# A diffusion transformer block on one core: gate modulation by quarters in the up projection, a written order at the end, input weights loaded one ahead

## The chip, the cores and the metric

The kernel runs on one core of a Trainium2 chip. The core has the TensorE (PE) for matmuls, the VectorE (DVE) and ScalarE (ACT) for elementwise work, the GpSimd (POOL, here almost only an issuer of DMAs) and the SyncE (SP, here only an issuer of DMAs), all of which run their own instruction streams in order and wait for each other by semaphores. The metric is the device time of one execution in microseconds (us). A profiled execution gives, beside it, every instruction with its start and its duration.

## What is computed

One layer of a hybrid diffusion backbone, for 512 latent tokens and 256 context tokens of width 2048, all in float32. Cut to what matters here:

```python
mod_l = silu(c) @ w_ada + b_ada              # 6 x 2048: sh_a, sc_a, gt_a, sh_f, sc_f, gt_f
mod_c = silu(c_ctx) @ w_ada + b_ada          # only sh_a, sc_a are needed
h_l = rms_norm(x, g_mix_norm) * (1 + sc_a) + sh_a
p   = h_l @ w_in                             # 3904 columns: attention and short conv
x   = x + gt_a * (merge_heads(att, conv) @ w_out)
h_f = rms_norm(x, g_ffn_norm) * (1 + sc_f) + sh_f
u   = dwconv3(h_f @ w_up)                    # 2 x 5504 columns
x   = x + gt_f * ((a * silu(g)) @ w_down)    # a, g = halves of u
out = rms_norm(x, g_final)
```

The modulation is six vectors of 2048 numbers for the latent tokens. In the kernel they are 96 tiles t of 128 numbers: 0 to 15 are sh_a, 16 to 31 sc_a, 32 to 47 gt_a, 48 to 79 sh_f and sc_f, and 80 to 95 gt_f, the gate behind the down projection.

## The kernel before

Features lie on the 128 partitions, tokens on the free axis. A float32 value is split into a rounded high part (cast on ACT) and the rest (subtracted on DVE), and each product is three matmuls: high by high, high by low, low by high (`mm3`, L183 to L185). So every weight block that comes by DMA costs a cast on ACT (L166, L984) and a subtraction on DVE (L167, L985) before the PE can use it. Tile names end in h and l accordingly.

The modulation is no matmul. A tile of 128 x 2048 of w_ada is loaded and multiplied on DVE with `sv`, the silu of c on all partitions, and summed along the row (a "dot"; two instructions of 128 x 1024 a tile, L229, L251, or four of 128 x 512, L1234). There are three places: `ada` (L229) in the input projection for t < 32, `late_dot` (L251) during attention and the out projection for t = 32 to 87, and `gate_mods` (L1234) in the first part of the down projection for t = 88 to 95, by quarters of 512, with `sv` read back from a DRAM copy `sv_d`. The context's own dots (L510) use `svc`, the silu of c_ctx.

The stages in order of time, with their rough place in the span:

- **Start** (0 to 28 us). SP issues the loads of c, the 16 tiles of x (xr), c_ctx, small constants, then w_ada and the first weights. `silu_rows` spreads c and c_ctx over all partitions by matmuls with ones and applies Silu on ACT (L393, L394). Squares of x are summed on DVE (15 adds, L335), `rms` turns them into the row `rl`: matmuls with ones (L300), square root on ACT (L277, with a load of its function table), reciprocal on DVE (L279), a transpose on the PE that spreads it (L284), a copy (L307). `modulate(j)` multiplies xs[j] by rl (L415), applies scale and shift on ACT (L418) and splits the result into h{j}h and h{j}l.
- **Input projection** (28 to about 600 with attention). w_in is taken in row chunks of 2, 4 and 10 tiles (`KCH`). In each chunk the first six column blocks (`pf`, weights `rf`) run beside the preparation of h; then the other 25 (`pp`, weights `rw`) follow, and each result is added into `acc` (L519, L521). A weight tile is loaded by `load` just where it is used, into one of two buffers of 1 MB (three with a spare one). The calls are written in program order, and `todo` says which h is prepared behind which block.
- **Out projection** (to about 808). Residual and squares of the new x tile by tile (`residual`, L943); the norm of the second half of the tokens waits for the last tile.
- **Up projection** (813 to 1676). The first three pairs of column blocks are done whole (`uf`), then for f = 3 to 42 a scheme of seven products (`product`, names p1, p2, p6, q5, p7 and q4, q3 of the round before, in `finish`) over 1024-wide weights `u`. Two of its five weight blocks are sums that the DMA makes by accumulating into SBUF (L1107). `acts` is the convolution and the gating, `pair_sums` (L1028 to L1047) makes sums of pairs and writes them out to `t_d`. Such background work lies in the queue `bg`, and `pump` takes one step of it behind each product. The rounds have nine weight buffers (`raw4`) and three split buffers each.
- **Down projection** (1676 to 2141). First seven tiles plainly (`d`), then 48 steps of seven products (`seven`, names v{st}p1 and so on) over windows of six pairs. `into` adds each result to its output tile `c` (L1319), from step 8 on times the gate. The last two steps, v22 and v23, are written out by hand.
- **End** (to 2156). Squares of the outputs, the final norm (L300, L277, L279, L284), `scale_out` (ACT, L1393) and `final`: the product with the norm on DVE (L1386) and the writes of 256 KB, 8 for each half of the tokens, issued from SP and ACT.

Within this code the framework's scheduler orders each engine's stream by priority in program order and modelled times, except where `keep` or an `issue_after` fixes one instruction behind another.

## Time and profile before

| | us |
|---|---|
| median of 3 runs | 2158.14 (2150.28 to 2158.75) |
| the profiled execution | 2158.0 |
| its span (first to last instruction) | 2156.2 |
| PE busy | 2104.1 |
| DVE busy | 1770.6 |
| ACT busy | 1046.8 |
| mean granted clock of the PE | 0.992 |

The span is what the trace shows from the first to the last instruction; 1.8 us of the execution lie outside it. The PE's busy time nearly fills the span, so the idle pieces, and the stretches with a granted clock below 1, are what to look at. The rows that matter are quoted in the prediction.

### The profile page before, as it was taken

The numbers are of one execution on the slowest core, as the hardware profiler recorded it, in microseconds if no ns is written. First come the engines' busy times: TensorE is split into PE (matmuls) and PEld (weight loads), VectorE is DVE, ScalarE is ACT, GpSimd is POOL, SyncE is SP. The second block draws the span as 40 slices with busy tenths as digits, with TensorE's granted clock in tenths as the row PEclk, the third lists the DMA queues.
The fourth block names the chain that finished last, engine by engine and source line by source line (L and its number), as shares of the span: only waits on it lengthen the run. The fifth ranks groups of instructions, "written<-read, shape, count | busy, mean of one in ns | idle before, by whom it ended". The sixth has DMA issues, their size and how long they took to land.

```text
span 2156.2 us, 37750 instructions
## 1 busy us (share of the span) xinstructions
PE 2104.1 (98%) x14458; PEld 1946.8 (90%) x14458; DVE 1770.6 (82%) x2859; ACT 1046.8 (49%) x1709; POOL 188.1 (9%) x270
## 2 busy tenths in 40 slices
PE   7999999999999999999999999999999999999996
PEld 4788788888988888999999999999999889999996
DVE  7998987778886989788888888788888659888886
ACT  5533333555542237555555555555555333333445
POOL 0000000000000000111111111111111000000000
PEclk9999999999999999999999999999999999999998
DMA  9989885334559986677877877887877998877773
GB/s 338 348 274 334 268 284 177 130 125 157 181 198 345 357 272 187 160 216 201 242 230 215 239 225 223 239 235 214 238 229 219 345 331 289 260 217 235 210 234 110
DMA packets 162409, 513.89 MB, mean 238 GB/s; under 512 B 18994, under 2 KB 23346, under 8 KB 156594
## 3 DMA queue, kind: packets, MB, share of 16 engines
q1 hardware_dynamic: 132564, 417.10, 56.7%
q0 software_dynamic: 27488, 92.29, 18.2%
q8 instruction: 113, 1.85, 0.3%
q10 hardware_dynamic: 2176, 2.10, 0.3%
q14 instruction: 68, 0.56, 0.1%
HBM read 464.22 MB, written 46.14 MB: 237 GB/s over the span
## 4 chain that ended last, share of the span: by engine, by line
PE 90%; DVE 4%; DMA 3%; ACT 2%; issue 1%; SPq 0%; DVEq 0%; ACTq 0%
PE pp L183 4%; PE pp L185 4%; PE pp L184 4%; PE o L183 1%; PE o L184 1%; PE o L185 1%; PE d L183 1%; PE d L185 1%; PE d L184 1%; PE uf L183 1%; DMA ada<-in_w_ada 1%; PE uf L184 1%; PE uf L185 1%; PE of L183 1%; PE of L184 1%; PE of L185 1%
## 5 line engine op out<-in xcount | busy, mean ns | idle before, releaser
L1030 POOL DMA_DIRECT2D t_d<-tp x126 | 71.8, 573 | 469.1 <-DVE tp L1029 466.7
L251 DVE SCALAR_TENSOR_TENSOR ada<-ada,sv 128x1024 f32<-128x1024 f32 x68 | 82.1, 1220 | 13.5 <-DMA ada<-in_w_ada 13.5
L166 ACT CAST w_0h<-rw 128x512 fp32r<-128x512 f32 (+1 forms) x63 | 38.3, 618 | 106.2 <-PE pp L184 65.4
L1107 POOL DMA_DIRECT2D u_s<-in_w_up x80 | 70.2, 877 | 225.2 <-DMA u_s<-in_w_up 109.8
L229 DVE SCALAR_TENSOR_TENSOR ada<-ada,sv 128x1024 f32<-128x1024 f32 x64 | 77.6, 1219 | 3.8 <-DMA ada<-in_w_ada 3.6
L510 DVE SCALAR_TENSOR_TENSOR ada<-ada,svc 128x1024 f32<-128x1024 f32 x64 | 76.0, 1220 | 2.8 <-DMA ada<-in_w_ada 2.8
L1028 ACT CAST tp<-a 128x256 fp32r<-128x256 f32 x90 | 34.7, 404 | 63.2 <-DMA t_d<-tp 51.8
L773 POOL TENSOR_TENSOR gr<-gr,half 128x8 f32<-128x8 f32 x4 | 10.1, 2522 | 627.8 <-DVE gr L772 535.8
L167 DVE TENSOR_TENSOR w_0l<-rw,w_0h 128x512 fp32r<-128x512 f32 (+1 forms) x63 | 42.6, 682 | 21.7 <-ACT w_0h L166 21.7
L251 DVE SCALAR_TENSOR_TENSOR ra<-ra,sv 128x1024 f32<-128x1024 f32 x44 | 52.5, 1219 | 1.4 <-DMA ra<-in_w_ada 1.3
L1199 DVE TENSOR_TENSOR u<-u,u_s 128x1024 f32<-128x1024 f32 x40 | 48.8, 1220 | 1.1 <-DMA u_s<-in_w_up 1.0
L1200 DVE TENSOR_TENSOR u<-u,u 128x1024 f32<-128x1024 f32 x40 | 48.7, 1218 | 0.0
L1029 DVE TENSOR_TENSOR tp<-a,tp 128x256 fp32r<-128x256 f32 x90 | 36.2, 418 | 13.8 <-ACT tp L1028 13.7
L744 ACT CAST pth<-t 128x384 fp32r<-128x384 f32 x64 | 28.6, 485 | 26.5 <-PE t L741 26.5
L521 DVE TENSOR_TENSOR acc<-acc,pp 128x512 f32<-128x512 f32 x50 | 34.0, 681 | 2.1 <-PE pp L185 2.1
L745 DVE TENSOR_TENSOR ptl<-t,pth 128x384 fp32r<-128x384 f32 x64 | 33.3, 550 | 2.7 <-ACT pth L744 2.7
L1028 ACT CAST tp<-ts 128x256 fp32r<-128x256 f32 x36 | 14.6, 407 | 41.5 <-DMA t_d<-tp 39.6
L725 DVE TENSOR_REDUCE mn<-s 128x1 f32<-128x768 f32 x32 | 30.4, 953 | 4.7 <-PE s L714 4.6
L1029 DVE TENSOR_TENSOR tp<-ts,tp 128x256 fp32r<-128x256 f32 x36 | 15.2, 422 | 22.3 <-ACT tp L1028 22.3
L991 ACT ACTIVATE g<-cg,sm 128x512 f32<-128x512 f32 x40 | 32.5, 813 | 0.6 <-DVE cg L1168 0.6
L991 ACT ACTIVATE a<-ca,sm 128x512 f32<-128x512 f32 x40 | 32.1, 803 | 0.0
L999 ACT ACTIVATE g<-g 128x512 f32<-128x512 f32 x43 | 27.1, 631 | 6.4 <-DVE g L993 6.4
(15965 smaller groups left out, 9401.3 us busy)
## 6 DMA issues: line engine op xcount, KB each, us to landing
ada<-in_w_ada SPq DMA_DIRECT2D x196, 512.0 KB, 6.0
u<-in_w_up SPq DMA_DIRECT2D x120, 512.0 KB, 8.3
w<-t_d SPq DMA_DIRECT2D x161, 256.0 KB, 5.3
u_s<-in_w_up SPq DMA_DIRECT2D x80, 512.0 KB, 4.2
u_s<-in_w_up POOLq DMA_DIRECT2D x80, 512.0 KB, 9.1
t_d<-tp POOLq DMA_DIRECT2D x126, 256.0 KB, 4.9
v<-in_w_dnw SPq DMA_DIRECT2D x72, 384.0 KB, 5.4
ra<-in_w_ada SPq DMA_DIRECT2D x22, 1024.0 KB, 4.9
```

Source lines behind the costliest of these rows:

```text
L183: PE.matmul(ps, w[0], x[0], start=first, stop=False, skip_group_check=on_top)
L184: PE.matmul(ps, w[0], x[1], start=False, stop=False, skip_group_check=on_top)
L185: PE.matmul(ps, w[1], x[0], start=False, stop=last, skip_group_check=on_top)
L229: V.scalar_tensor_tensor(out=r, in0=r, scalar=1.0, in1=vec[:, i * 1024:(i + 1) * 1024], op0=ALU.mult, op1=ALU.mult, accum_out=col[:, i:i + 1])
L251: keep(V.scalar_tensor_tensor(out=r, in0=r, scalar=1.0, in1=svs[i], op0=ALU.mult, op1=ALU.mult, accum_out=lc[:, t % 4:t % 4 + 1] if i else ...
L510: keep(V.scalar_tensor_tensor(out=raw[q], in0=raw[q], scalar=1.0, in1=svc[:, q * 1024:(q + 1) * 1024], op0=ALU.mult, op1=ALU.mult, accum_o ...
L991: A.activation(u, src, AF.Identity, bias=s("fb", m), scale=s("fw", 86 + m))
L1028: A.copy(out=z[:, :256], in_=src)
L1029: V.tensor_tensor(out=z[:, 256:], in0=src, in1=z[:, :256].bitcast(F32), op=ALU.subtract)
L1030: G_.dma_start(t_d[p, OPS.index(n)], z.bitcast(F32))
L1107: G_.dma_start(r[-1], src[more], accum_op=ALU.add)
L1199: V.tensor_tensor(out=a11, in0=a11, in1=s1, op=ALU.add)
```

## The change

Three groups of edits.

**Modulation.** `late` ends at tile 80 instead of 88, so eight tiles (16 dots, 8 MB) leave the out projection. `gate_mods` now covers all 16 gate tiles and is stepped in the up projection: `product` calls `between`, which takes a step of `bg` or, where none waits, the next quarter. There are 64 loads of 256 KB and 64 dots of 128 x 512, through one buffer (tag "ts", shared with the temporary of `pair_sums`), and rl is reused for the quarter of sv. The down projection's 32 quarters and their four loads of sv are gone. sv_d is written in the out projection instead of right at the start.

**Input projection.** The silu of c_ctx leaves the start: c_ctx is loaded on all partitions and goes through one Silu of 128 x 2048 in the second chunk. The squares make two sums of eight tiles, with 14 adds. The first dots (tiles 16 and 0) and the first scaling are put in a written order around the reciprocal. Weights come from `weights()`, which issues the load after the one that it hands out, ahead of the `modulate` and `prep` calls that follow.

**End.** The a12 and s3 of the last step get buffers of their own, a square root of a constant is put on ACT behind the casts of q4, and outs, squares and statistics are fixed in one written order; the first half's writes are all issued from SP.

```diff
-    late = {"t": 32, "raw": None, "end": 88}
+    late = {"t": 32, "raw": None, "end": 80}
...
+        def prep_first():
+
+            a = first_dot(1, 0, recips[0].ins)
+            with tc.issue_after(a):
+                b = V.tensor_tensor(out=xs[0], in0=xs[0], in1=rl, op=ALU.mult).ins
+            first_dot(1, 1, b)
+            low_after[:] = [total(first["col"][1], 0, mod[:, 0:1]).ins]
...
-        silu_rows(c_ctx, svc, "cc")
         fetch_to(sm, small)
-        rms([ssq], D, T, rl)
+        first_scale()
+        ahead.append(first["last"])
+        rms(sqs, D, T, rl)
...
+        def weights(ahead=True):
+
+            raw = ready.popleft()
+            if ahead:
+                load_next()
+            return raw
...
-                    prep(q)
+                    prep(q) if q else prep_first()
+                    if q:
+                        load_next()
...
-                    raw = load(w_in[:, off:off + 2 * G * P], 2 * G * P, f"rf{ci}{q}")
+                    raw = weights(ci > 0)
...
+    def gate_mods():
+
+        for q in range(4):
+            SP.dma_start(rl, sv_d[:, q * T:(q + 1) * T])
+            for i in range(16):
+                r = cp.tile([P, T], F32, tag="ts", bufs=1, name=f"aq{i}{q}")
+                SP.dma_start(r, w_ada[80 + i][:, q * T:(q + 1) * T])
+                yield
+                V.scalar_tensor_tensor(out=r, in0=r, scalar=1.0, in1=rl, op0=ALU.mult, op1=ALU.mult, accum_out=parts[q // 2][:, i, q % 2:q % 2 + 1])
...
+    def between():
+
+        if bg:
+            pump(1)
+        else:
+            next(gm, None)
+
     def product(ps, a, n, nm, first):
...
-        pump(1)
+        between()
...
+        own = ("12", "s3") if st == STEPS - 1 else ()
...
+    with tc.issue_after(last_hi[0]):
+        A.activation(tiny(1, "root"), eps, AF.Sqrt)
+    pump(1)
+    d_q5(za, (3,))
     squares(za.m + 1, H1)
-    pump(2)
-    d_q5(zb)
+    d_q5(zb, (1,), lambda: [keep(next(outs)) for _ in range(2)])
+    keep(last_into[0])
     squares(zb.m + 1, H1)
-    pump(1)
     scaled = {j: scale_out(j, 1) for j in range(0, za.m, 2)}
-    for _ in range(3):
-        next(outs)
+    keep(next(outs))
     d_q3(za)
```

How the streams move, at three places. SP at the start, from the first weights on; before (rf and rw are weights of w_in, ada modulation loads, sv_d the copy of sv):

```order
L145 DMA rf_251<-in_w_in 128x1536
L972 DMA sv_d<-sv 128x2048
L145 DMA ada_283<-in_w_ada 128x1024
L145 DMA ada_285<-in_w_ada 128x1024
L145 DMA ada_291<-in_w_ada 128x1024
L145 DMA ada_293<-in_w_ada 128x1024
L145 DMA rw_13_337<-in_w_in 128x2048
L145 DMA ada_360<-in_w_ada 128x1024
L145 DMA ada_362<-in_w_ada 128x1024
```

Six further ada loads follow there, and then the second load rw. After (here all weights of w_in are named rw):

```order
L145 DMA rw_226<-in_w_in 128x1536
L145 DMA ada_274<-in_w_ada 128x1024
L145 DMA ada_276<-in_w_ada 128x1024
L145 DMA ada_282<-in_w_ada 128x1024
L145 DMA ada_284<-in_w_ada 128x1024
L145 DMA rw_298<-in_w_in 128x2048
L145 DMA rw_330<-in_w_in 128x2048
L145 DMA ada_353<-in_w_ada 128x1024
L145 DMA ada_355<-in_w_ada 128x1024
```

The second and the third rw now stand together behind the first four ada loads that follow the first weights, and the copy of sv is gone from this place.

DVE in the up projection, in the round f = 7 (g, a, ca, cg are convolution and sums, names in l the low parts); before:

```order
L318 TENSOR_TENSOR yh5l<-a_9248,yh5h 128x512
L1200 TENSOR_TENSOR u_12_9109<-u_12_9109,u_11_9107 128x1024
L985 TENSOR_TENSOR u6q4l<-u_22_8870,u6q4h 128x1024
L1210 SCALAR_TENSOR_TENSOR ca_9123<-u6c,u_9345 128x256
L985 TENSOR_TENSOR u6q3l<-u_12_8862,u6q3h 128x1024
L1198 TENSOR_TENSOR cg_9363<-u7b,u_9393 128x256
L985 TENSOR_TENSOR u7p6l<-u_11_9107,u7p6h 128x1024
L985 TENSOR_TENSOR u7q5l<-u_s_9111,u7q5h 128x1024
L1168 TENSOR_TENSOR cg_9122<-u6c,u_9286 128x256
L985 TENSOR_TENSOR u7p7l<-u_s_9114,u7p7h 128x1024
```

After, the same piece with the quarter dots aq:

```order
L1247 SCALAR_TENSOR_TENSOR aq_9754,modc<-aq_9754,rl 128x512
L338 TENSOR_TENSOR yh5l<-a_9213,yh5h 128x512
L1069 TENSOR_TENSOR u6q3l<-u_12_8812,u6q3h 128x1024
L1311 TENSOR_TENSOR cg_9328<-u7b,u_9361 128x256
L1069 TENSOR_TENSOR u7p6l<-u_11_9060,u7p6h 128x1024
L1247 SCALAR_TENSOR_TENSOR aq_9787,modc<-aq_9787,rl 128x512
L1069 TENSOR_TENSOR u7q5l<-u_s_9064,u7q5h 128x1024
L1281 TENSOR_TENSOR cg_9075<-u6c,u_9251 128x256
L1069 TENSOR_TENSOR u7p7l<-u_s_9067,u7p7h 128x1024
L1076 SCALAR_TENSOR_TENSOR g_9461<-cg_9075,sm,g_9461 128x511
L1076 SCALAR_TENSOR_TENSOR a_9466<-ca_9076,sm,a_9466 128x511
L1247 SCALAR_TENSOR_TENSOR aq_9818,modc<-aq_9818,rl 128x512
```

Three dots stand in this piece, each on the same buffer, so that the load for one is issued behind the dot before it; the splits keep their order among each other.

ACT in the last steps, around v23p6h, which the PE needs first of v23's later products (out are the scalings of finished output tiles); before:

```order
L1393 ACTIVATE out_23729<-c_18805,sm 128x256
L1393 ACTIVATE out_23729<-c_18807,sm 128x256
L1393 ACTIVATE out_23732<-c_18809,sm 128x256
L1393 ACTIVATE out_23732<-c_18811,sm 128x256
L1393 ACTIVATE out_23735<-c_18813,sm 128x256
L1393 ACTIVATE out_23735<-c_18815,sm 128x256
L1393 ACTIVATE out_23738<-c_19124,sm 128x256
L1393 ACTIVATE out_23738<-c_19126,sm 128x256
L1393 ACTIVATE out_23741<-c_19130,sm 128x256
L984 CAST v23p6h<-v_23326 128x768
L984 CAST v22p7h<-v22s_23132 128x768
L984 CAST v23p7h<-v23s_23329 128x768
```

After:

```order
L1490 ACTIVATE out_23766<-c_18893,sm 128x256
L1490 ACTIVATE out_23769<-c_18895,sm 128x256
L1490 ACTIVATE out_23769<-c_18897,sm 128x256
L1490 ACTIVATE out_23772<-c_18899,sm 128x256
L1490 ACTIVATE out_23772<-c_18901,sm 128x256
L1490 ACTIVATE out_23775<-c_18903,sm 128x256
L1068 CAST v23p6h<-v_23360 128x768
L1490 ACTIVATE out_23775<-c_18905,sm 128x256
L1490 ACTIVATE out_23778<-c_19172,sm 128x256
L1490 ACTIVATE out_23778<-c_19174,sm 128x256
L1068 CAST v22p7h<-v22s_23166 128x768
L1490 ACTIVATE out_23781<-c_19178,sm 128x256
```

Before, 15 scalings stand between v21q3h and v23p6h; after, 11 do, and the others follow it.

164 lines of the change are left out of this document (105 added, 59 removed).

## The prediction

> **What bounds the kernel now.** I read the page's first part, then the busy time in stretches, then the waits of the PE, and last the rows around the long waits.
>
> ```profile
> PE 2104.1 (98%) x14458; PEld 1946.8 (90%) x14458; DVE 1770.6 (82%) x2859; ACT 1046.8 (49%) x1709; POOL 188.1 (9%) x270
> ```
>
> The PE has work in all but 2156.2 - 2104.1 = 52.1 us of the span. No matmul of the model's layers is removed by the change, so all that it can win is a part of these 52 us, and time in which the PE runs at a lower clock. The stretches (PE, PEld, DVE, ACT, POOL busy, then granted clock, DMA share, GB/s) say where they lie:
>
> ```profile
> 0.00:20.00 20.00, 12.24 (x14) 4.34 (x15) 11.19 (x19) 14.81 (x25) 0.20 (x4) 1.00 0.91 329
> 20.00:40.00 20.00, 15.29 (x44) 9.71 (x44) 17.59 (x36) 9.09 (x15) 0.00 (x0) 1.00 0.93 367
> 40.00:60.00 20.00, 16.92 (x72) 13.16 (x71) 17.31 (x36) 10.28 (x19) 0.00 (x0) 1.00 0.93 337
> 60.00:80.00 20.00, 17.69 (x75) 13.45 (x74) 17.87 (x37) 11.66 (x22) 0.00 (x0) 1.00 0.88 309
> 80.00:100.00 20.00, 18.61 (x81) 14.79 (x80) 19.69 (x40) 13.72 (x25) 0.00 (x0) 1.00 1.01 400
> 100.00:120.00 20.00, 20.00 (x88) 16.22 (x87) 20.00 (x38) 5.07 (x8) 0.00 (x0) 1.00 0.82 286
> ...
> 220.00:240.00 20.00, 18.03 (x82) 14.48 (x82) 18.97 (x38) 6.39 (x11) 0.00 (x0) 1.00 0.80 262
> ...
> 800.00:820.00 20.00, 15.99 (x110) 15.46 (x109) 17.54 (x42) 11.03 (x24) 1.08 (x2) 0.83 0.89 321
> ...
> 960.00:980.00 20.00, 20.00 (x169) 20.00 (x168) 15.46 (x19) 10.96 (x16) 2.86 (x4) 1.00 0.78 210
> ...
> 2110.00:2120.00 10.00, 6.06 (x36) 5.42 (x36) 6.78 (x9) 10.00 (x24) 0.00 (x0) 0.81 0.39 79
> 2120.00:2130.00 10.00, 10.00 (x74) 10.00 (x74) 6.45 (x12) 4.65 (x8) 0.00 (x0) 0.84 0.01 2
> ```
>
> The first five rows lack 100 - 80.75 = 19.25 us; the passage from the out projection to the up projection (800 to 820) lacks 4.0, the last steps of the down projection (2110 to 2120) 3.9. The middle of the up projection lacks nothing, and the DVE has 4.5 us free there in 20. Three rows at and after a long wait show a clock below 1. The waits of the PE name the causes:
>
> ```profile
> PE pp L183 <- ACT acc L519: 6.8, 6, 1.6
> ...
> PE v23a L183 <- ACT v23p6h L984: 3.6, 1, 3.6
> PE pf L183 <- ACT h0h L317: 3.2, 1, 3.2
> ...
> PE rs L300 <- DVE fq0t L335: 3.0, 1, 3.0
> ...
> PE pp L185 <- DVE w_0l L167: 2.0, 1, 2.0
> ```
>
> **Start: 5.5 us gained.** Rows of ACT, DVE, PE and SP's DMA issues:
>
> ```profile
> 23.09 1.28 ACT L277 ACT_TABLE_LOAD   x1
> ...
> 52.06 0.62 ACT L166 CAST w_0h<-rw 128x512 fp32r<-128x512 f32 x1 [5.51 <-DMA rw<-in_w_in]
> ```
>
> ```profile
> 19.29 1.22 DVE L229 SCALAR_TENSOR_TENSOR ada<-ada,sv 128x1024 f32<-128x1024 f32 x1
> ...
> 27.00 0.69 DVE L415 TENSOR_TENSOR xr<-xr,rl 128x512 f32<-128x512 f32 x1
> ```
>
> ```profile
> 29.24 2.08 PE L183 MATMUL pf<-h0h,wf_0h 128*128 128x512 f32 x4 [3.21 <-ACT h0h L317]
> ```
>
> ```profile
> 43.59 0.38 SPq L145 DMA_DIRECT2D rw<-in_w_in  x1
> ```
>
> Before, the table of the square root is loaded at 23.09, behind the four Silu pieces of c_ctx, and xs[0] is scaled by rl only at 27.00, behind four dots and three weight splits. In the new order the Silu is gone from here, the reciprocal stands behind the second dot, the scaling behind the third, the weight splits behind the fourth. Walked: two dots from 19.29 end at 21.7, the third at 23.0, the scaling (0.69) at 23.7, the fourth dot and its sum at 25.1. From the end of the scaling to the first matmul, activation and cast, are 29.24 - 27.69 = 1.55 now, so that matmul comes near 26.7: 2.5 gained; bounds 0 (if a load is late) and 3.2 (the whole wait). The second rw load stood behind eight modulation loads and was issued at 43.59; now it stands right behind the first and is issued before 30. The 5.51 us of ACT go, and with them two of the six waits for acc, the longest 1.6 by its row: I take 3.0; bounds 0 and 6.8 (all six). The write of sv (1 MB) leaves the start as well, where the DMA share is 0.91; it lies among the x loads of the out projection now, at no cost that I can see in its rows. The Silu of c_ctx returns later, on ACT, with two table loads (1.28 each): in 100 to 120 ACT works 5 us of 20, which hides it; uncovered it would cost some 4 us.
>
> **Out projection to up projection: 4.6 us gained.**
>
> ```profile
> 808.56 1.23 DVE L251 SCALAR_TENSOR_TENSOR ada<-ada,sv 128x1024 f32<-128x1024 f32 x1 [0.36 <-DMA ada<-in_w_ada]
> ...
> 810.11 0.48 DVE L943 SCALAR_TENSOR_TENSOR x<-ol,mod,x 128x256 f32<-128x256 f32 x1
> ```
>
> The last residual starts at 810.11 only because the last modulation dot (waiting for its load) and two sums stand ahead of it: DVE was free for it at 808.56 - 0.36 = 808.2, and 810.11 - 808.2 = 1.9 us. Tiles 80 to 87 leave this stretch (16 dots of 1.23, 8 MB), so the wait of 3.0 for fq0t shrinks by 1.9 to about 1.1. The lower clock costs 15.99 x 0.17 = 2.7 in this row. Waits of 3.0 and 3.6 us are followed by it; that of 2.0 (row 220 to 240, clock 1.00) is not. With 1.1 left I expect it to stay at 1.00. Sum 1.9 + 2.7 = 4.6; bounds 0 and 3.0 + 2.7 = 5.7.
>
> What the Trainium skill says of this stands in "TensorE: Matmul & The Clock Gate", Part 1: a window without work of about 3.4 us halves the clock, and about 3.4 us of work bring it back. By it a remaining wait between 2 and 3 us, which no row decides, would keep the clock too, while this case already shows the loss at 3.0.
>
> **Up projection: 2 us lost.** 64 dots and 64 loads of 256 KB move into it, one buffer for all, so each load starts when the dot before it is done. They bring 16 MB to SP's queue; SP's u loads wait for buffers that DVE frees, and the aq issues stand in that same order. Ahead of the nearest rows for dot and landing (the down projection before), then DVE in one round, then the PE's first use of u7q4l:
>
> ```profile
> L1234 DVE SCALAR_TENSOR_TENSOR aq<-aq,svq x32: 683/687/693, 1703.2 to 1788.1; 128x512 f32<-128x512 f32 x32
> ...
> DMA to landing us min/median/max: 4.3/6.0/7.2
> ```
>
> ```profile
> 962.74 1.23 DVE L985 TENSOR_TENSOR u6q3l<-u,u6q3h 128x1024 fp32r<-128x1024 f32 x1 [0.48 <-ACT u6q3h L984]
> ...
> 965.57 1.23 DVE L985 TENSOR_TENSOR u7p6l<-u,u7p6h 128x1024 fp32r<-128x1024 f32 x1 [0.47 <-ACT u7p6h L984]
> 968.45 1.23 DVE L985 TENSOR_TENSOR u7q5l<-u_s,u7q5h 128x1024 fp32r<-128x1024 f32 x1 [1.65 <-ACT u7q5h L984]
> ...
> 973.13 0.74 DVE L992 SCALAR_TENSOR_TENSOR a<-ca,sm,a 128x511 f32<-128x511 f32 x1
> ...
> 980.87 1.21 DVE L985 TENSOR_TENSOR u7q4l<-u,u7q4h 128x1024 fp32r<-128x1024 f32 x1
> ```
>
> ```profile
> 984.80 0.28 PE L185 MATMUL u7a<-T40h,u7q4l 128*128 128x256 f32 x1
> ```
>
> 64 dots over some 23 rounds of 20 us are 2.8 a round: 2.8 x 0.69 = 1.9 us, of 4.5 free. In the order one stands ahead of u6q3l, one behind u7p6l, one behind that 511-wide a. Between the first and the second lie about 4.0 us (962.8 to 966.8), then 6.4 (967.5 to 973.9), then some 8. A load that lands in 4.3 costs 0.3 a round; in 6.0, 2.0 and more. The 2.6 left swallow either at first, and u7q4l is ready 984.80 - 982.08 = 2.7 ahead of its use. The DMA share here is 0.78, where those landings were taken in a fuller stretch, so I choose the near end, 4.3 to 5: 2 us in all for single waits; bounds 0 and the rival below. A load of half an ada tile pays the fixed part of a transfer oftener. In the Trainium skill, "DMA: Bandwidth & Descriptors", Anatomy of one DMA, a transfer takes about 2.0 us and its bytes at 436 GB/s, an estimate of 2.6 us here and a loss of 0; the landings above are longer, so the trace disagrees.
>
> The down projection loses 32 dots and 36 loads, where the PE lacked 1 us at most: 0.
>
> **End: 7.4 us gained.** ACT, DVE, PE:
>
> ```profile
> 2104.63 0.84 ACT L984 CAST v23p2h<-v 128x768 fp32r<-128x768 f32 x1 [4.89 <-DMA v<-in_w_dnw]
> ...
> 2110.04 6.09 ACT L1393 ACTIVATE out<-c,sm 128x256 f32<-128x256 f32 x15
> 2116.04 0.81 ACT L984 CAST v23p6h<-v 128x768 fp32r<-128x768 f32 x1
> ```
>
> ```profile
> 2114.19 0.96 DVE L1329 TENSOR_TENSOR v<-v,v23s 128x768 f32<-128x768 f32 x1 [2.67 <-DMA v23s<-in_w_dnw]
> ...
> 2139.26 3.69 DVE L1386 TENSOR_TENSOR out<-out,rl 128x512 f32<-128x512 f32 x6
> 2142.87 0.48 DVE L1319 SCALAR_TENSOR_TENSOR c<-v23c,mod,c 128x256 f32<-128x256 f32 x1
> ```
>
> ```profile
> 2140.68 0.28 PE L185 MATMUL v23c<-w,v23q3l 128*128 128x256 f32 x1
> ```
>
> Buffers of their own for a12 and s3 of the last step start both loads and the add sooner, which takes away DVE's 2.67 and ACT's 4.89. ACT still has 11 scalings instead of 15 ahead of v23p6h: 4 x 0.41 = 1.6, and it begins them earlier by perhaps 0.7 to 1.5. The wait of 3.6 shrinks by 2.3 (bounds 1.6 and 3.1) and leaves about 1.3, below the 2.0 that kept the clock: 6.06 x 0.19 + 10 x 0.16 = 2.75 more (bound 0). In the tail the last c waits from 2140.96 to 2142.87 behind six outs; in the written order three stand there and two behind: 1.8. Of the two outs left over one goes ahead of the last chain: 0.6. The square root's table is loaded early in either case off the path. Sum 2.3 + 2.75 + 1.8 + 0.6 = 7.4; bounds 1.6 and 8.3.
>
> **Sum.** 2158.0 (profiled execution: span 2156.2 and 1.8 around it; the runs' median is 2158.14) - 5.5 - 4.6 + 2 - 7.4 = 2142.5.
>
> **Rivals.** First, the other side: DVE becomes the bound in the up projection. If the loads land in 6.0 us at every tight spacing, the waits are 2.0 and 1.8 a round (the second spacing shrinks to 4.2 once DVE has no free time), and 3.8 + 1.9 = 5.7 stands against 4.5 free: 1.2 x 23 = 27 us, 2169.5. It decides from about 5.4 us. Against it: DMA share 0.78, and landings late in a round have 6 to 8 us; for it: one buffer, and the row's median. Chance 0.20, half of it above 2168.9, where slower begins.
>
> Second, the waits shrink but the clock still falls in both places: +2.7 + 2.75 gives 2148. For it speaks that no row lies between 2.0 and 3.0. Chance 0.16.
>
> Third, the start's gain is swallowed: DVE is full from 100 to 120, and the PE waits 2.0 for it near 223, so what is won by then may wait there. 2142.5 + 5.5 = 2148. This is also the case in which the early load merely delays the modulation loads behind it. Chance 0.14.
>
> **How the numbers follow.** The forecast has 0.50, its own range 2136 to 2148. About 0.5%, 10.8 us, is what a measurement here can tell from no change: 2147.4 to 2168.9. Faster: 0.48 + 0 + 0.05 + 0.07 = 0.60; slower: 0.10 from the first rival and 0.01 from the third; the rest, 0.29, the same. The range runs from 2133 (all bounds at their good ends, 10 + 5.7 + 8.3 off, and one more) to 2163, leaving out 0.07 below and 0.12 above.
>
> **What would show it.** First main matmul at 26 to 27, no 5 us wait of ACT for rw near 52; rs waiting about 1 us for fq0t and a clock of 1.00 at 800 to 840; DVE near 18 of 20 in the up projection with the PE at 20.00; v23a waiting under 2 us with clock 1.00 behind it; the last c within 0.3 of its last matmul. Wrong would be PE below 20.00 in many stretches of the up projection, with DVE waiting for aq.

## The result, and the profile after

The changed kernel takes **2259.9 us** (median of 4 runs, 2257.43 to 2273.39) against 2158.44 for the kernel before in the same comparison (4 runs, 2150.28 to 2161.53): ratio 1.0486, 95% interval 1.0455 to 1.0518. Forecast were 2142.5 and a range up to 2163. The PE's busy time rose by 19.8 us, but its share of the span fell from 98 to 94%. The first part of the page after:

```profile
PE 2123.9 (94%) x14458; PEld 1961.7 (87%) x14458; DVE 1770.8 (79%) x2887; ACT 1046.4 (46%) x1709; POOL 187.8 (8%) x270
```

Where the time lies is read from the first matmul of two products, the first of round 3 and of round 42 of the up projection (before, then after; the fields are line, engine, instruction, duration in ns, first and last start):

```profile
L183 PE MATMUL u3a<-hf0h,u3p1h x1: 288/288/288, 883.8 to 883.8; 128*128 128x256 f32 x1
```

```profile
L183 PE MATMUL u42a<-hf0h,u42p1h x1: 281/281/281, 1661.4 to 1661.4; 128*128 128x256 f32 x1
```

```profile
L193 PE MATMUL u3a<-hf0h,u3p1h x1: 288/288/288, 877.7 to 877.7; 128*128 128x256 f32 x1
...
L193 PE MATMUL u42a<-hf0h,u42p1h x1: 280/280/280, 1767.1 to 1767.1; 128*128 128x256 f32 x1
```

Up to round 3 the change is 6.1 us ahead. From round 3 to 42 it takes 889.4 us instead of 777.6: **111.8 lost**. The rest of the span is 488.6 instead of 494.8, 6.2 won. 111.8 - 6.1 - 6.2 = 99.5, the difference of the spans (2255.7 - 2156.2). Everything that needs explaining lies in the up projection. The whole piece from round 3 to 42 in one row, before and after (columns as in the prediction):

```profile
883.80:1661.40 777.60, 777.60 (x6482) 777.60 (x6481) 644.22 (x851) 446.47 (x665) 137.40 (x204) 1.00 0.79 225
```

```profile
877.70:1767.10 889.40, 810.31 (x6481) 800.91 (x6480) 681.36 (x979) 443.34 (x665) 137.16 (x204) 0.96 0.74 215
```

Before, the PE never stands still there. After, it is idle for 889.4 - 810.3 = 79.1 us, and its mean granted clock is 0.96 instead of 1.00, which costs by estimate another 0.04 x 889.4 = 36 us. The two come to some 3 us more than the loss, which the last section bears on. Single stretches after:

```profile
1060.00:1080.00 20.00, 20.00 (x170) 20.00 (x170) 15.67 (x23) 10.42 (x15) 1.06 (x2) 1.00 0.76 215
1340.00:1360.00 20.00, 12.10 (x80) 11.89 (x79) 10.04 (x14) 7.73 (x14) 1.80 (x4) 0.74 0.57 177
1640.00:1660.00 20.00, 14.34 (x113) 13.72 (x113) 14.27 (x21) 10.77 (x18) 4.52 (x7) 0.98 0.81 232
1700.00:1720.00 20.00, 16.05 (x124) 16.05 (x125) 13.98 (x19) 9.33 (x16) 3.95 (x6) 0.91 0.64 181
```

Some stretches are full, in others the PE lacks 4 to 8 us of 20, and in those no engine is full: DVE works 10 to 14 us. So it is not a bound by DVE's work. The dots and their landings (tile aq), the waits of DVE, of ACT and of the PE (us in total, times, longest):

```profile
L1247 DVE SCALAR_TENSOR_TENSOR aq<-aq,rl x64: 678/691/695, 856.9 to 1451.3; 128x512 f32<-128x512 f32 x64
...
DMA to landing us min/median/max: 3.0/4.7/11.5
```

```profile
DVE tp L1113 <- ACT tp L1112: 83.3, 34, 8.1
DVE aq L1247 <- DMA aq<-in_w_ada: 75.6, 32, 5.7
```

```profile
ACT tp L1112 <- DMA t_d<-tp: 145.9, 51, 10.4
```

```profile
PE u24a L193 <- ACT u24p1h L1068: 7.9, 1, 7.9
...
PE u27a L193 <- ACT u27p1h L1068: 5.4, 1, 5.4
...
PE u39a L193 <- ACT u39p1h L1068: 4.0, 1, 4.0
```

The last dot starts at 1451.3, in round 28, but u39a waits 4.0 us long after it, and rounds 29 to 41 lose 30.9 us in all. The dots cannot be their direct cause. The PE waits mostly for a product's cast on ACT, and ACT for the **folds**: `pair_sums` casts seven tiles tp for each pair of rounds, POOL writes each to t_d, and two buffers are left for the tp, so a cast of tp waits until the tp two before has been written.

### The profile page after: what moved, and what is told of

It is laid out like the page before. It is cut to its first block, busy times and chain, and to the rows that moved or that the text cites. A ratio compares the mean times of both kernels' runs of the same rounds, so it can differ in the third digit from the quotient of the medians.

```text
span 2255.7 us, 37763 instructions
## 1 busy us (share of the span) xinstructions
PE 2123.9 (94%) x14458; PEld 1961.7 (87%) x14458; DVE 1770.8 (79%) x2887; ACT 1046.4 (46%) x1709; POOL 187.8 (8%) x270
## 4 chain that ended last, share of the span: by engine, by line
PE 57%; DMA 23%; DVE 11%; issue 5%; ACT 2%; POOL 1%; SPq 0%; DVEq 0%; POOLq 0%; ACTq 0%
DMA aq<-in_w_ada 8%; DMA t_d<-tp 7%; PE pp L193 4%; PE pp L195 4%; PE pp L194 4%; DMA u_s<-in_w_up 3%; PE o L195 1%; PE o L194 1%; PE o L193 1%; PE d L193 1%; DMA ofr<-in_w_out_first 1%; PE d L195 1%; PE d L194 1%; DMA ada<-in_w_ada 1%; PE pf L193 1%
## 5 line engine op out<-in xcount | busy, mean ns | idle before, releaser
L1114 POOL DMA_DIRECT2D t_d<-tp x126 | 77.1, 627 | 426.5 <-DVE tp L1113 404.5
L1247 DVE SCALAR_TENSOR_TENSOR aq<-aq,rl 128x512 f32<-128x512 f32 x64 | 44.1, 689 | 75.8 <-DMA aq<-in_w_ada 75.6
L240 DVE SCALAR_TENSOR_TENSOR ada<-ada,sv 128x1024 f32<-128x1024 f32 x60 | 72.5, 1220 | 1.9 <-DMA ada<-in_w_ada 1.6
L262 DVE SCALAR_TENSOR_TENSOR ada<-ada,sv 128x1024 f32<-128x1024 f32 x52 | 62.8, 1220 | 11.7 <-DMA ada<-in_w_ada 11.7
L169 DVE TENSOR_TENSOR w_0l<-rw,w_0h 128x512 fp32r<-128x512 f32 (+1 forms) x63 | 42.7, 684 | 22.7 <-ACT w_0h L167 18.5
```

Of the source, the lines that this page charges most:

```text
L240: V.scalar_tensor_tensor(out=r, in0=r, scalar=1.0, in1=vec[:, i * 1024:(i + 1) * 1024], op0=ALU.mult, op1=ALU.mult, accum_out=col[:, i:i + 1])
L262: keep(V.scalar_tensor_tensor(out=r, in0=r, scalar=1.0, in1=svs[i], op0=ALU.mult, op1=ALU.mult, accum_out=lc[:, t % 4:t % 4 + 1] if i else ...
L1114: G_.dma_start(t_d[p, OPS.index(n)], z.bitcast(F32))
```

## The experiments

The theories at first: S, the buffer "ts" that quarters and folds share; L, the quarters' loads and DVE's waits for them; T, the dots' time on DVE. After four runs a fourth came, **P**: the quarters change the order in which the folds' casts stand among the products' casts on ACT, and this order lasts. The table gives, for the first matmul of a round, how many us later it starts than before, both counted from round 3. All kernels but the kernel before have the change's edits of start and end.

| run | time, us | round 10 | 17 | 28 | 42 |
|---|---|---|---|---|---|
| changed kernel | 2259.9 | 13.1 | 21.2 | 72.3 | 111.8 |
| e1 modulation undone | 2155.2 | 0.1 | 0.0 | 0.0 | 0.0 |
| e2 64, own buffer | 2219.7 | 9.7 | 32.1 | 53.2 | 75.4 |
| e3 64 dots, no loads | 2201.7 | 1.7 | 15.7 | 30.9 | 54.6 |
| e4 64 loads, 4 small dots | 2249.7 | 36.7 | 64.2 | 80.7 | 101.4 |
| e5 32 dots | 2137.7 | 1.9 | 0.2 | -2.2 | -5.4 |
| e6 48 dots | 2195.5 | 0.6 | 8.8 | 27.4 | 49.2 |
| e7 24, own buffer | 2209.4 | 12.1 | 24.7 | 40.2 | 64.0 |
| e8 32, shared buffer | 2172.6 | 14.3 | 27.3 | 28.7 | 28.7 |
| e9 e6, place written | 2145.5 | 0.8 | 6.0 | 3.6 | 0.4 |
| e10 e2, place written | 2209.3 | 11.0 | 58.6 | 68.8 | 65.6 |
| e11 changed, place written | 2270.6 | 12.2 | 57.1 | 125.6 | 125.5 |
| e12 e11, about every other place | 2207.9 | 3.5 | 11.5 | 36.7 | 60.4 |
| e13 32 eighths, place written | 2177.0 | 15.0 | 29.4 | 27.0 | 24.4 |
| e14 e13, place not written | 2224.1 | 18.5 | 39.0 | 54.6 | 76.3 |
| e15 48 in the down projection | 2163.0 | 0.0 | 0.0 | 0.0 | 0.0 |
| e16 16 eighths far apart | 2150.0 | 0.0 | 0.0 | 0.0 | 0.0 |
| e17 e16, the whole computation | 2150.5 | 0.1 | 0.0 | 0.1 | 0.0 |

The times of the changed kernel, e1, e11, e12, e13, e15, e16 and e17 are medians of 4 to 10 runs, the others are single runs. The rounds are those of one profiled execution each.

**e1: modulation undone.** `late` ends at 88 again, `between` is `pump(1)` again, the 32 quarters lie in the down projection.

> The changed kernel with the modulation part undone: gate tiles 80 to 87 by late dots in the out projection and 88 to 95 by quarters in the down projection, as before; the start's order, the weights one ahead and the written end stay. If the up projection's quarters are the whole loss: 2147 to 2152 us (start about -2, end about -6), no PE stretch in the up projection below 19.9 of 20. If the end or the start has a part in the loss, or if the order of the folds in the up projection falls behind for another reason: above 2165.

2155.17 against 2157.36 before, ratio 0.9992 (0.9981 to 1.0004): no difference that can be measured, and each round of the up projection as before to 0.1 us. The whole loss belongs to the modulation. The time lies 3 us above the range expected: in this profile the end wins 5.8 us, as expected, but the start wins nothing (round 3 at 884.6, before 883.8).

**e2, e3, e4: buffer, dots and loads apart.**

```
e2  -   r = cp.tile([P, T], F32, tag="ts", bufs=1, name=f"aq{i}{q}")
    +   r = rl
e3  -   SP.dma_start(r, w_ada[80 + i][:, q * T:(q + 1) * T])
    +   V.scalar_tensor_tensor(out=rl, in0=rl, scalar=1.0, in1=rl, ...)
e4  +   SP.dma_start(rl, w_ada[80 + i][:, q * T:(q + 1) * T])
    -   V.scalar_tensor_tensor(out=r, in0=r, scalar=1.0, in1=rl, ...)
    +   V.scalar_tensor_tensor(out=rl[:, :16], ...)      # once behind 16 loads
```

> The changed kernel with the 64 quarters loaded into rl, a buffer that nothing else uses in this stage, instead of the buffer tag shared with the sums of pairs; the dot multiplies the quarter by itself, so the gate's values differ, and the four loads of sv are left out. All 64 loads and dots stay, still one buffer, each load behind the dot before it. Theory S (the sharing makes the pair sums wait for the quarters, so that they fall behind and are then caught up too densely for their two write buffers): 2145 to 2160, the pair sums in step again. Theory L (DVE waits for the landing of each quarter in its one buffer, 75.6 us in the changed kernel): 2215 to 2245, DVE still waits 60 us or more for aq. Theory T (DVE time or DMA traffic of the 64 quarters): 2240 to 2260.

> The changed kernel with the 64 dots at their places but no loads of w_ada for them: each dot works on rl in place (multiply and maximum with itself), so the gate's values are left out. Theory S: 2140 to 2148. Theory L: 2140 to 2148. Theory T with DVE time as the cost: 2180 or more; with DMA traffic as the cost: 2140 to 2148.

> The changed kernel with the 64 quarter loads into rl but without the dots (the gate's values are constants), so that the traffic of 16 MB on SP's queue stands alone. Theory S: 2140 to 2148. Theory L: 2140 to 2148, since nothing waits for the loads. Theory T with DMA traffic as the cost (u loads and their accumulation land later): 2180 or more.

None of the three theories fits all three runs. Without the shared buffer 75.4 us are lost, without loads 54.6, with loads and four small dots 101.4. L has e2's time right (2215 to 2245, though with 44.7 us of waits for the quarters instead of 60 or more) and T those of e3 and e4 (2180 or more), but S and L put e3 below 2150, and T put e2 at 2240 or more. S has a part all the same: with the shared buffer 111.8 us are lost instead of 75.4, so 36.4 more (e2 also leaves out four loads of sv). In e3 the last dot starts at 1075.2, as round 13 begins; 3.0 us were lost by then, and 51.6 come afterwards, in rounds whose instructions are those of before. Of e4, ahead of round 15, the waits of SP's queue and of DVE, and the small dots:

```profile
SPq L1243 <- DMA rl<-in_w_ada: 208.1, 58, 6.8
```

```profile
DVE rl L1245 <- DMA rl<-in_w_ada: 32.6, 4, 15.8
DVE u L1312 <- DMA u_s<-in_w_up: 30.1, 5, 8.5
```

```profile
L1245 DVE SCALAR_TENSOR_TENSOR rl<-rl x4: 175/176/177, 916.6 to 1139.6; 128x16 f32<-128x16 f32 x4
```

Between the small dots nothing reads the loads, and they go out one behind the other's landing into one buffer; SP waits for each, and the weights for the sums u_s stand behind them. But DVE also waits 32.6 us in the four small dots, and in the rounds where they stand (4, 7, 10 and 13) the PE waits for splits behind them. So e4 doesn't show what loads alone cost.

**Theory P.** In e3 the products' casts keep their order, but behind the last dot the folds stand elsewhere among them: their casts on ACT, with them their steps on DVE and their writes on POOL, and some matmuls of the PE change places too. ACT's instructions around rounds 34 and 35 in the kernel before, then in e6 (48 dots, which differ from e3 in number alone); the sources of the products' casts are left off, and g and a are put in one row:

```
before  L1028 CAST tp_16190<-ts_16034      e6  L1068 CAST u34q5h
        L984 CAST u34q5h                       L1278 ACTIVATE ca
        L1166 ACTIVATE ca                      L1112 CAST tp_16187<-ts_16031
        L1028 CAST tp_16225<-a_16001           L1068 CAST u34p7h
        L984 CAST u34p7h                       L1075 ACTIVATE g, a
        L991 ACTIVATE g, a                     L1112 CAST tp_16222<-a_15998
        L984 CAST u35p1h                       L1068 CAST u35p1h
```

Six of a pair's seven fold casts stand one product later in e6, in this pair and in every one from rounds 13 and 14 to rounds 37 and 38: the scheduler orders the streams ahead of time, by its own reckoning of when things are ready, and comes out in another regular pattern once the dots have pushed the folds. In the changed kernel the folds even fall behind, by up to 35 products, which is five rounds, with the pair of rounds 21 and 22, and come back only with that of 35 and 36, into the shifted pattern of e6. This order can be read without running anything; with 32 dots (e5) it is that of before, with 48 (e6) it is shifted, and with 32 quarters in the shared buffer (e8) it is that of before from round 18 on. P and the theory that the loss goes with the number of dots or quarters (D) then part clearly.

```
e5      for i in range(8):      # 16 in e3
e6      for i in range(12):
e7      for i in range(6):      # e2 otherwise
e8      for i in range(8):      # the changed kernel otherwise
```

> As the dots-only kernel (no quarter is loaded, each dot runs on the one buffer rl), but 32 dots instead of 64, one a step, so that they end at about half the time (near 930 to 970). Leaves out: the gate's modulation itself (its value is meaningless). In the program the folds' casts on ACT stand at the same products as before the change (last cast of a pair ahead of the second product of the third round after it). Theory P (any quarter that shifts the folds' casts against the products' casts costs 1.7 to 2 us a round from there to the stage's end, and the dots themselves cost little): no shift here, so 2150 to 2162, as the kernel with the modulation undone (2155). Theory D (the dots' time on DVE, and the loss lasts once it is made; in proportion to their number): half of the 46 us of the 64 dots, so 2173 to 2183.

> The same with 48 dots. Leaves out the same. In the program the folds' casts are shifted by one product from the third pair on, to the stage's end, as with 64 dots. Theory P: 2190 to 2205, the same as with 64 dots (2201.7), up to the stage's end some 45 us later than before, nearly all of it after the first eight rounds. Theory D: 48/64 of 46 us, 2185 to 2193. Together with the run with 32 dots: P a step of 35 us or more between them, D a step of about 12.

> As the kernel with loads and dots in a buffer of their own (64 of them: 2219.7), but 24 loads and dots. Leaves out: the gate's modulation itself (each quarter is multiplied by itself, 24 instead of 64). In the program the folds' casts are shifted by one product from the first pair on. Theory P: rounds from the 17th on lose about 39 us in all as with 64; with some 5 to 12 us for the quarters themselves 2190 to 2207. Theory D (proportional to loads and dots): 24/64 of 64 us, 2175 to 2182.

> The changed kernel with 32 quarters instead of 64, in the buffer that it shares with the folds. Leaves out: half of the gate's modulation. In the program the folds lag in the first four pairs and stand as before the change from the fifth pair (round 18) on, to the stage's end. Theory P: what is lost in rounds 4 to 17 (15 to 25 us), nothing from round 18 on: 2165 to 2182, less than the run with 24 quarters of their own. Theory D: half of the changed kernel's 104.7 us, 2200 to 2212, more than that run.

P's forecasts hold in e6 and e8, D's in none (in e6 D is out by 2.5 us only); e7 is 2 us above P's 2207; e5 is 12 us below P's 2150 and far from D's. Sixteen dots more cost 57.8 us (e6 over e5), while 32 quarters through the shared buffer cost less than 24 in one of their own. From round 18 on, e8 loses nothing. The price of the shift, from rounds 17 to 42, is 40.4 us in e6 and -5.6 in e5: 46.0 in 25 rounds, 1.8 a round. These are single runs, but the steps are far larger than the scatter of the kernels that were run several times (16 us at most).

**e9 to e12: the place written out.** The casts of five products in two rounds are issued behind the fold's cast that stands ahead of them before the change; no instruction is added.

```
+    AHEAD_OF = {"p1": "1", "p6": "22", "q5": "2", "p7": "21"}, {"p2": "4"}
-        last_hi[:] = [A.copy(out=hi[:, :n], in_=src).ins]
+        with tc.issue_after(behind_fold) if behind_fold is not None else ExitStack():
+            last_hi[:] = [A.copy(out=hi[:, :n], in_=src).ins]
-            A.copy(out=z[:, :256], in_=src)
+            fold[p, n] = A.copy(out=z[:, :256], in_=src).ins
-        w = split4(a, 1024, nm)
+        w = split4(a, 1024, nm, fold.get((f // 2 - 5, AHEAD_OF[f % 2].get(k))))
e12 -        else:
    +        elif free[0] % 7 in (0, 2, 4, 6):     # counts the places without a step of bg
```

> As the run with 48 dots (2195.5), with the same instructions; only the place of the folds' casts on ACT is written out (the product casts p1, p6, q5, p7 of each even round and p2 of each odd round are issued behind one named cast of the fold), so that they stand as before the change. Leaves out the gate's modulation itself. Theory P (the place of the folds' casts): 2135 to 2145, as the run with 32 dots (2137.7), and no loss of more than 5 us by the last round. Theory D (the dots and their time on DVE): unchanged, 2190 to 2200.

> As the kernel with 64 loads and dots in a buffer of their own (2219.7), with the folds' casts in the written place. Leaves out the gate's modulation itself (each quarter is multiplied by itself). Theory P: what stays is only what the loads and dots cost in the first 13 rounds, 10 to 15 us: 2147 to 2158. Theory D: 2210 to 2225.

> The changed kernel whole, with the folds' casts in the written place. Theory P: the 40 us of the last 14 rounds go and most of the shift before; what stays are the waits for quarters that share one buffer with the folds, by the run with 32 quarters some 0.9 us each, so at most 57 us: 2160 to 2200. Theory D: 2245 to 2265.

> The same with a quarter in four of seven free places (mostly every other one) instead of in each, so that a load has two products (5.7 us) to land instead of one (2.9). Theory P with the landings of 3.0/4.7/11.5 us: a part of the waits for quarters is left, 10 to 25 us: 2147 to 2165, below the run with a quarter in each place by 10 us or more. Theory D (the loss goes with the number of quarters): as that run, within 5 us.

e9 settles the dots: the same instructions as e6, 2145.5 instead of 2195.5 us. **The order alone is worth 50 us.** Only ACT's order was written, but with it, from round 16 on, the other engines' streams are as before too, so the 50 us are those of all of them. The 48 dots cost 7.6 us by round 11, in e9; that only 0.4 are left by round 42 comes from the closer matmuls of the last section. How it costs shows ACT's timeline at the first product of round 35 (start, duration, in brackets the idle time ahead and its releaser), in e6 and in e9:

```profile
1546.24 0.80 ACT L1075 ACTIVATE a<-ca,sm 128x512 f32<-128x512 f32 x1
1551.27 0.41 ACT L1112 CAST tp<-a 128x256 fp32r<-128x256 f32 x1 [4.23 <-DMA t_d<-tp]
1551.58 1.04 ACT L1068 CAST u35p1h<-u 128x1024 fp32r<-128x1024 f32 x1
```

```profile
1512.43 0.80 ACT L1079 ACTIVATE a<-ca,sm 128x512 f32<-128x512 f32 x1
1513.61 1.05 ACT L1072 CAST u35p1h<-u 128x1024 fp32r<-128x1024 f32 x1 [0.38 <-PE u34a L194]
...
1517.64 0.41 ACT L1116 CAST tp<-a 128x256 fp32r<-128x256 f32 x1 [2.71 <-DMA t_d<-tp]
```

In e6 the cast that the PE needs next stands behind a fold's cast that waits 4.23 us for a write; in e9 the write's wait of 2.71 lies behind that cast, and the PE doesn't wait. The write is late for a reason in the order, too. POOL's issues for the same folds, in e6 and in e9:

```profile
1538.96 0.56 POOL L1114 DMA_DIRECT2D t_d<-tp  x1 [14.30 <-DVE tp L1113]
1540.51 0.87 POOL L1191 DMA_DIRECT2D u_s<-in_w_up  x1 [1.00 <-DMA u_s<-in_w_up]
1541.08 0.86 POOL L1114 DMA_DIRECT2D t_d<-tp  x1
```

```profile
1503.70 1.13 POOL L1118 DMA_DIRECT2D t_d<-tp  x2 [12.02 <-DVE tp L1117]
1507.22 0.89 POOL L1195 DMA_DIRECT2D u_s<-in_w_up  x1 [2.40 <-DMA u_s<-in_w_up]
```

The pair's second write stands right behind an accumulating load of u_s in e6 and lands after 10.2 us, when the tp cast at 1551.27 can start; in e9 it stands ahead of that load and lands after 5.7. Of the 126 writes 46 take more than 8 us in e6, 23 in e9 and 25 before. The PE's wait list between 1200 and 1660 is empty in e9, and in e6 it names the first cast of every odd round:

```profile
PE u39a L193 <- ACT u39p1h L1068: 2.6, 1, 2.6
...
PE u35a L193 <- ACT u35p1h L1068: 2.3, 1, 2.3
```

Behind 10 of the 13 waits of this kind from 1160 on the granted clock falls, so that the 1.8 us a round are made of wait and clock. The row of round 35 in e6:

```profile
1552.00:1574.00 22.00, 21.33 (x166) 21.33 (x167) 18.30 (x25) 12.93 (x20) 3.93 (x6) 0.92 0.72 204
```

But e10 (2209.3) and e11 (2270.6) came out far above P's numbers and refute it as the only cause; they lie within 1 and 6 us of D's ranges, which e9 has refuted for the dots. Their rounds lose nothing once the last quarter is done (e11: 125.6 at round 28, 125.5 at 42), and lose more while quarters run: e11 is no better than the changed kernel (ratios 1.0518, 1.0487 to 1.0549, and 1.0486, 1.0455 to 1.0518, both to before). e11 and e10 differ in the buffer (and four loads of sv): with the order written, sharing it with the folds costs 125.5 - 65.6 = 59.9 us by round 42. Waits of e10 between 990 and 1170, of the PE, of DVE and of ACT:

```profile
PE u12c L193 <- ACT u12q5h L1072: 7.1, 1, 7.1
PE u10c L193 <- ACT u10q5h L1072: 6.5, 1, 6.5
```

```profile
DVE rl L1250 <- DMA rl<-in_w_ada: 28.6, 15, 4.9
```

```profile
ACT tp L1116 <- DMA t_d<-tp: 25.2, 7, 6.5
...
ACT tp L1116 <- DVE a L1125: 9.3, 3, 5.5
```

DVE stands at a dot whose quarter has not landed, the fold's steps on DVE stand behind it, the tp cast and its write behind those, and the product's cast, now in a fixed place, behind the next tp cast, which waits for that write (6.5 us ahead of u12q5h). With quarters in about every other place (e12) half of the loss goes: 2207.9, outside the 2147 to 2165 expected of it. So a second theory is W: beside the place, quarters lose time where DVE meets them before they have landed.

**e13 to e17: loads with time to land.** e13 leaves tiles 80 to 83 in the out projection and puts 84 to 87, by eighths, in a buffer of their own, into every third free place; e14 is the same without the written place; e15 has no quarter in the up projection.

```
e13 +   SP.dma_start(rl[:, :256], sv_d[:, e * 256:(e + 1) * 256])
    +   r = rl[:, 256:]
    +   SP.dma_start(r, w_ada[84 + i][:, e * 256:(e + 1) * 256])
    +   if free[0] % 3 == 0: next(um, None)
e15 -   for i in range(8):            +   for i in range(12):      # from w_ada[84]
    -   for _ in range(2):            +   for _ in range(3):       # quarters a step
```

> Tiles 80 to 83 stay in the out projection and 88 to 95 in the down projection, as before the change; only tiles 84 to 87 lie in the up projection, as 32 eighths (128x256) in a buffer that the folds don't use, one in every third free place, and the folds' casts stand in the written place; the edits of start and end stay. Theory W (beside the folds' place, quarters lose time only where DVE has to wait for their landing): a load has at least 8 us to land, so no waits, the up projection loses 0 to 3 us, and the passage wins 10 to 15 us against the kernel with the modulation undone (2155): 2138 to 2148, faster than both kernels. Theory B (every load costs by its traffic or by holding SP's queue; 71 us for 64 loads in the run with a buffer of their own and written casts, so 0.5 to 1.1 each): 16 to 35 us lost, 2156 to 2180.

> The same without the written place of the folds' casts; in the program they are shifted by one product from the first pair on. Theory P: 45 to 55 us more than with it. Against P: the same time within 5 us.

> No modulation in the up projection: tiles 80 to 83 in the out projection, 84 to 95 as 48 quarters in the down projection, three a step in its first part instead of two; start and end as in the changed kernel. Theory W: DVE has 7 to 12 us of 20 free there and two or more buffers, so nothing is lost beside the 10 to 15 us won in the passage: 2140 to 2150. Theory B: 16 more loads of 256 KB in a stretch whose DMA share is about 1 cost 0.7 us each: 2150 to 2162.

e14 took 47.1 us more than e13 and shows P with loads: from round 17 to 42 it loses 37.3 us and e13 gains 5.0. e13's price fits B and not W (2138 to 2148), but it did not test W: the dots ran from 865.4 to 1049.0, all 32 in the first eight rounds, since the scheduler drew them forward, and DVE waited for them:

```profile
DVE rl L1250 <- DMA rl<-in_w_ada: 32.6, 14, 7.1
```

e15 missed by 13 us: ratio 1.0022 (1.0003 to 1.0040). Its rounds of the up projection are those of before, but in the down projection, with 16 more quarters, the PE waits 3.3 us for one y tile and 2.6 for a split. e16 leaves the written place out and holds each dot in its place, behind the split of the product written last:

```
+                with tc.issue_after(last_split[0]):
                     V.scalar_tensor_tensor(out=r, in0=r, scalar=1.0, in1=rl[:, :256], ...)
+   if free[0] % 6 == 0: next(um, None)       # tiles 86 and 87 only; late ends at 86
```

> The modulation whole: tiles 80 to 85 in the out projection, 86 and 87 in the up projection as 16 eighths (128x256) in a buffer that the folds don't use, 88 to 95 in the down projection; start and end as in the changed kernel. In e13 the eighths were not far apart: the scheduler had drawn all 32 into the first eight rounds, where DVE still waited 32.6 us for them. Here each dot is issued behind the split of a product six free places after its load, so that one comes about every two rounds, and the folds' casts stand as before the change without being written out. Theory W (DVE's waits for the landing, which folds and casts behind them inherit): no wait for a load, and no round longer than before: the up projection within 5 us of before, and with 4 to 6 us won in the passage 2146 to 2153. Theory B (each load costs by its traffic or SP's queue): 16 loads of half the size at 0.5 to 1.0 us, 8 to 16 us lost in the up projection: 2158 to 2168.

> As e16, with the last sums of tiles 84 and 85, which e16 left out (late totals are made every four tiles; here also at the last one): two DVE additions of some 0.1 us more ahead of the passage. Computes the whole reference. Theory W as e16 showed it: no round of the up projection longer than before, 2147 to 2153, ratio to before 0.995 to 0.998, below both kernels. If the two sums on the way to the last residual cost more than their time: 2153 to 2157.

W's forecasts hold, B's does not: no round is longer than before. The dots and the PE's only wait between 880 and 1690 in e16:

```profile
L1248 DVE SCALAR_TENSOR_TENSOR rl<-rl x16: 417/418/422, 958.8 to 1549.6; 128x256 f32<-128x256 f32 x16
```

```profile
PE d L193 <- ACT dw00h L1068: 1.0, 1, 1.0
```

That is also the only wait there of the kernel before, and no dot waits for its load. e16 (which leaves out the last sums of tiles 84 and 85) takes 2150.0 us, ratio 0.9966 (0.9953 to 0.9979); e17, the whole computation, **2150.45 us** (2142.93 to 2154.32) against 2157.41 before, ratio **0.9956** (0.9938 to 0.9973). So it is 0.4% faster than the kernel before, and some 110 us faster than the changed one. e16 and e17 put 2 MB into the up projection, where the change put 16, and their folds stand as before without being written. They show that loads and dots cost nothing there when no dot waits and the order stays; that all 64 quarters could be placed so, no run shows.

## Why the prediction was wrong, step by step

**Up projection, 2 us lost: measured 111.8. This is the step that failed.** The sum weighed the dots' work and two landings against DVE's free time in a round, 4.5 us in 20, and let the remaining 2.6 "swallow either at first". The landings were as chosen in the median (4.7, chosen 4.3 to 5, with 11.5 as the longest), and DVE's busy time hardly changed. But the waits for them were 75.6 us in 32 times, nearly 3 us a round up to round 28, where the sum had 0.3 to 1.0. And four things were missing. First, the sum treated a wait of DVE as a withdrawal from slack, while DVE's instructions stand in order: behind a dot that waits stand the folds' steps, behind these ACT's tp casts with their two buffers and their writes, and behind these the product's cast that the PE needs (the waits of e10 read as that chain, and in e16, where no dot waits, it is gone). Second, the order was looked at on DVE in one round, where the splits kept their order, and not on ACT and POOL, where the folds' casts and writes moved past products, to the end of the stage (e6 against e9, 50 us). Third, that quarters and folds hold back each other through the one buffer had no term (36.4 us by e2, 59.9 by e10 and e11). Fourth, the clock had none in this stage: 0.96 over it, by estimate 36 of the 111.8 us, against 1.00 before. How the rest splits is not settled: these mix, since the waits also decide what a shift costs.

The 2.6 us for a landing that the prediction works out from the Trainium skill ("DMA: Bandwidth & Descriptors", Anatomy of one DMA) lies below the shortest of the 64, 3.0. The section that it names gives its figures for transfers issued by GpSimd, and these are issued by SP.

**The first rival** named the right stage, side and buffer, and the wait for aq was there (75.6 us in 32 times). Its mechanism, DVE as the bound from landings of 5.4 us on, was not: DVE's share fell from 82 to 79%, and the landing's median stayed below its point. Its 27 us were a quarter of what came. (Its sum counts the forecast's 2 us as well; without them it is 2167.5, not 2169.5.)

**Start, 5.5 us gained.** The first main matmul came at 27.40 (forecast 26.7), and by the first blocks of the second row chunk 3.2 us were won. ACT's wait for rw near 52 is gone, but the waits for acc fell only from 6.8 to 6.1, where 3.0 less had been forecast. At the attention 0.8 were left. The third rival (the gain is swallowed) had this right: the PE waited 2.4 for w_0l (at 220.6), and the clock fell behind it.

```profile
200.00:220.00 20.00, 18.27 (x80) 14.48 (x78) 18.84 (x34) 5.75 (x10) 0.00 (x0) 1.00 0.88 321
220.00:240.00 20.00, 19.36 (x81) 15.74 (x82) 19.33 (x36) 5.49 (x10) 0.00 (x0) 0.91 0.86 288
```

**Out to up projection, 4.6 gained.** From the start of the out projection's last blocks to round 3 it took 95.6 us instead of 99.3: 3.7 won, and 1.6 more lay ahead of that. The wait for fq0t fell from 3.0 to 1.6 (forecast 1.1), but the clock did not stay at 1.00:

```profile
800.00:820.00 20.00, 18.01 (x138) 17.72 (x137) 14.73 (x41) 14.07 (x32) 1.08 (x2) 0.91 0.77 260
```

Shorter rows of the same place show what such a mean stands for:

```profile
805.00:809.20 4.20, 2.21 (x18) 1.92 (x17) 2.98 (x10) 3.75 (x9) 0.54 (x1) 1.00 0.93 277
809.20:812.50 3.30, 3.30 (x17) 3.30 (x17) 3.30 (x7) 3.30 (x8) 0.00 (x0) 0.50 0.93 314
812.60:820.00 7.40, 7.40 (x64) 7.40 (x64) 5.29 (x18) 4.02 (x11) 0.00 (x0) 1.00 0.82 285
```

The clock is halved for some 3.4 us and full on both sides, behind 2.0 us without work in 4.2. Here the Trainium skill's rule ("TensorE: Matmul & The Clock Gate", Part 1: about 3.4 us without work) does not fit the trace: no single wait was above 1.6 us.

**Down projection 0, end 7.4 gained.** From the down projection's first matmul on 6.0 us were gained. v23a waits 1.7 us (forecast 1.3) and the clock behind it is 1.00, as forecast; the last c stands 0.1 us behind its last matmul instead of 1.9, and within 0.3 was forecast.

```profile
2210.00:2220.00 10.00, 8.14 (x67) 7.74 (x65) 6.70 (x11) 10.00 (x25) 0.00 (x0) 1.00 0.20 67
2220.00:2230.00 10.00, 9.05 (x74) 8.88 (x75) 8.14 (x13) 8.85 (x17) 0.00 (x0) 1.00 0.01 2
```

Without the piece from round 3 to 42 the change wins 12.3 us of the span in these two executions, where 17.5 were forecast.

## What to carry to other kernels

Work that is to fill an engine's gaps must be ready when the engine reaches it: in an in-order stream a wait for a load is passed on to the chains behind it, and here free time in the average did not pay for it. A buffer shared with such a chain adds to it. Where a scheduler orders the streams, compare the order on every engine of the stage, to its end, and not only where the new work stands; a shift of one place that looks like nothing cost 1.8 us a round. Such an order can be compared before anything is run, and a few written places (e9), or work far enough apart (e17), keep it.

## What the runs showed that was not expected

The clock falls behind short waits: to 0.50 for some 3.4 us with no wait above 1.6 us (809 after), and to a mean of 0.74 around the wait of 7.9 us for u24p1h (1340 to 1360). The length of a single wait does not decide it: in e6 the clock falls behind one of 1.8 us (at 1508.7) and not behind one of 2.4 (at 1596.8).

In e5, e9, e10 and e13 the rounds without loss run some 0.2 us faster than before (e5: -5.4 by round 42) with no wait of the PE in either and a granted clock of 1.00 in both: 171 matmuls in 20 us instead of 169. Rows of e1, of e5 and of e6:

```profile
1400.00:1420.00 20.00, 20.00 (x169) 20.00 (x168) 16.10 (x22) 12.04 (x18) 3.37 (x5) 1.00 0.84 241
```

```profile
1400.00:1420.00 20.00, 20.00 (x171) 20.00 (x171) 16.34 (x21) 11.12 (x16) 2.41 (x5) 1.00 0.78 216
```

```profile
1574.00:1594.00 20.00, 20.00 (x171) 20.00 (x170) 15.18 (x21) 9.46 (x14) 3.41 (x5) 1.00 0.73 209
```

Where the PE runs without a wait, the matmuls of a round start 120.0 ns apart in the mean, or 118.7. In the kernel before, e1, e15, e16 and e17, whose PE never waits in these rounds, it is 120.0 throughout. In the other runs it changes between the two, and 118.7 is the value of most rounds of the changed kernel and of e6, where the waits hide it, and of many of e8's up to round 17. So e6 and e9 may be compared, while a comparison of such a run with the kernel before is too good by some 0.2 us a round: 7 to 8 us in e5's and e9's times, and the 3 us by which idle time and clock came out above the loss have the same sign. Its cause is open.
